# A SwiGLU feed-forward's first product as seven quarter products per block, on x without its norm

## The chip, the core and the metric

The program runs on one core of one Trainium2 chip. The metric is the device time of one execution in microseconds. TensorE does the matmuls into PSUM banks; VectorE (DVE), ScalarE (ACT) and GpSimd (POOL) do everything that is elementwise; the DMAs are issued from SyncE (SP).

## What is computed

Two layers of a decoder trunk on 528 tokens (16 learned ones and 512 of the input) of 1024 channels. Each layer is a feed-forward, a token-mixing part and a second feed-forward, each with an RMS norm before and behind it:

```python
h = h + 0.5 * rms_norm(swiglu(rms_norm(h, g[0]), w_in, w_out), g[1])
...                                   # token mixers: attention, convolution, recurrence, sparse attention
h = h + 0.5 * rms_norm(swiglu(rms_norm(h, g[4]), w_in, w_out), g[5])

def swiglu(x, w_in, w_out):
    gate, up = jnp.split(x @ w_in, 2, axis=-1)
    return (jax.nn.silu(gate) * up) @ w_out
```

`w_in` is 1024 x 5120 and `w_out` 2560 x 1024, all float32. There are four feed-forwards; below they are numbered 1 to 4 in order of time.

## The kernel before

**Numbers.** Activations lie with channels on partitions and tokens in the free dimension: eight tiles of 128 channels, 528 tokens each. A float32 number is used as two float32r parts, hi and lo = value - hi, and a product is hi\*hi + hi\*lo + lo\*hi: three matmuls per 128 channels. The tokens are cut into two halves of 264 columns (256 in feed-forward 4, which drops the learned tokens). So one weight block of 128 output columns costs 8 x 3 = 24 matmuls a half.

**The first product.** The 2560 hidden channels are 20 blocks `j` of 128; a block needs a gate block and an up block of `w_in`. `weight` fetches 1024 columns into a `wraw` buffer (two of them), `wsplit` copies hi on ScalarE (`whi` or `wh`) and subtracts lo on VectorE (`wlo` or `wl`). Three pairs from a pool and three from rings of the mixers (`SPARE`) make six hi/lo pairs that are used in turn. `x` is h times the norm's column of gains; the norm's factor of each token, `R`, is only known later and is multiplied in behind the product. `gated` does that for a half: gate bank times R on VectorE (`ga`), SiLU on ScalarE, up bank times R on VectorE, gate times up on GpSimd, then hi on ScalarE and lo on VectorE into a tile `G`. Blocks 0 to 2 are the lead: they are done at the end of the phase before (`lead`), woven into other work. In feed-forward 4 both halves make one 512-column product in blocks 3 to 19.

**The second product.** The blocks are taken in chunks of 6, 6 and 8 (`CHUNKS`). Behind each chunk its 8 output blocks of 128 channels are made of its `G` tiles and added up in `y`. The last chunk's are the `tail`, woven with the beginning of the next phase; `link` there makes the norm of `y` (`leave`) and the next `x` (`enter`). Feed-forward 4 ends with tokens on partitions instead (`ffn_out_tokens`).

**What sets the order.** Blocks 3 to 19 stand in the program in plain order, and the tile framework's scheduler places each engine's instructions. Tail, mixers and lead are woven by hand: streams are taken by a planner that keeps times per engine (`Weave`), ranks (`RANK`) and a choice of engine per task (`ENG`, `SUMS`); that order is then fixed for TensorE, ScalarE, VectorE and GpSimd. Nearly all instructions carry the line of the recording helper, 252, so the rows are told apart by tile names. Eight PSUM banks stand in three groups: `psu` (2), `psa` (5) and `psn` (1).

Of the kernel before, what the change touches and what calls it, by code (L numbers as in the profile page):

```python
# [9 lines left out]
F32 = mybir.dt.float32  # L10
# [6 lines left out]
P = 128  # L17
# [90 lines left out]
class Weave:  # L108
# [13 lines left out]
    AHEAD = dict(PE=0.0, A=0.19, V=0.0, G=0.3)  # L122
# [255 lines left out]
class Trunk:  # L378
# [6 lines left out]
    LEAD = 3  # L385
    WB = 3
# [6 lines left out]
    ENG = dict(hadd='V', wlead='E', wt='V', wcol='G', wearly='G', wlate='V', wtail='V', wnext='E', gelu='G',  # L393
               geluo='V', gate='G', ct='V', tapsum='E', rfox='E', rconv='V', rlru='E', rdsa='G', lrua='V',
               lrub='E', lruc='V', lrud='V', lrut='G')
    KEPT = ("PE", "A", "V", "G")
    RANK = dict(ev=6.3, late=48.5, weights=10.8, row=100.5, lead=49.3, index=217.3, prep=150.7, scores=13.7,
                dsa=144.3, topk=153.4, fox=42.6, lru=14.4, lrub=59.1, first=81.6, turn0=0, turn1=168.8,
                start0=47.9, start1=229.5, leading=184.0, conv=0, column=99.8, link=0, enter=80.0,
                tail=13.0, small=9.3, next=117.2)  # L400
# [336 lines left out]
    def leave(self, y, acc, c, l, s, factor):  # L737
# [4 lines left out]
        self.norm_rows(acc, R, self.NORMS[0], factor)  # L742
# [30 lines left out]
    def gated(self, G, pg, pu, R, c):  # L773
        nc = self.nc
        w = c.stop - c.start
        tiles = self.tmp(name="ga", many=2)
        t, u = (i[:, :w] for i in tiles)
        nc.vector.tensor_mul(t, pg[:, :w], R[:, c])
        nc.scalar.activation(t, t, AF.Silu)
        nc.vector.tensor_mul(u, pu[:, :w], R[:, c])  # L780
        nc.gpsimd.tensor_mul(u, u, t)
        nc.scalar.activation(G[:, 0, c], u, AF.Copy)
        nc.vector.tensor_sub(G[:, 1, c], u, G[:, 0, c].bitcast(F32))
        self.drop(*tiles)

# [48 lines left out]
    def ffn(self, l, f, w, state, final):  # L834
# [5 lines left out]
        params = self.load_params() if not (l or f) else iter(())  # L840
        for ch, cj in enumerate(CHUNKS):
            base = sum(CHUNKS[:ch])
            Gs = [(self.led[j], 0) for j in range(self.LEAD)] if not ch else []
            for j in range(base + len(Gs), base + cj):
                G = self.at(self.Y[j % 8], [P, 2, T], F32R, name="G")
                ws = [self.weight(wi[:, :, o + j * P : o + (j + 1) * P], KB, P) for o in (0, DFF)]
                next(params, None)
                groups = [[self.half(0, w), self.half(1, w)]] if 2 * w <= 512 else [[self.half(i, w)] for i in range(2)]
                for group in groups:
                    banks = [self.pu(), self.pu()]  # L850
                    for p, hl in zip(banks, ws):
                        self.product(p, hl, KB, x, slice(group[0].start, group[-1].stop))
                    for i, c in enumerate(group):
                        self.gated(G, *(p[:, i * w : (i + 1) * w] for p in banks), R, c)
                Gs.append((G, 0))
            if final:
                self.ffn_out_tokens(l, 5 if f else 1, ch, base, cj, wo, Gs)
# [19 lines left out]
    def tail(self, name, l, f, w, rest, state, pre):  # L877
# [37 lines left out]
        def link(half):  # L915
            wv.wait(f"{name}y{half}")
            c = self.half(half, w)
            update = self.leave(y, sums[half][0], c, l, 5 if f else 1, 0.5)
# [7 lines left out]
    def ffn_out_tokens(self, l, s, ch, base, cj, wo, Gs):  # L926
# [5 lines left out]
        if not ch:  # L932
            self.yt = [self.at(r, [P, D], name="yt") for r in ("fk", "qd", "gl", "cv0")]
            self.grow = self.at("xb", [P, D], name="grow")
            nc.sync.dma_start(self.grow, self.a["norm_g"][l, s].partition_broadcast(P))
        last = ch == len(CHUNKS) - 1
# [1051 lines left out]
```

## Time and profile before

| | us |
|---|---|
| median of 3 runs (2100.37 to 2101.22) | 2100.42 |
| the profiled execution, its own time | 2100.15 |
| its span, first to last instruction | 2098.4 |
| TensorE busy in it | 1989.9 |
| VectorE, ScalarE, GpSimd busy | 1223.5, 900.0, 487.6 |

The span divides into feed-forwards, where TensorE runs without a gap, and the two mixing phases (about 345 to 775 us and 1390 to 1788 us) and one plain link of two feed-forwards (1040 to 1093 us), where all engines share the work. A TensorE instruction's recorded length is longer than its turn, since matmuls follow each other in a pipeline: the turn is a window's length divided by the matmuls in it.

### The profile page before, as it was taken

The numbers are of one execution on the slowest core, as the hardware profiler recorded it, in microseconds if no ns is written. First come the engines' busy times: TensorE is split into PE (matmuls) and PEld (weight loads), VectorE is DVE, ScalarE is ACT, GpSimd is POOL, SyncE is SP. The second block draws the span as 40 slices with busy tenths as digits, with TensorE's granted clock in tenths as the row PEclk, the third lists the DMA queues.
The fourth block names the chain that finished last, engine by engine and source line by source line (L and its number), as shares of the span: only waits on it lengthen the run. The fifth ranks groups of instructions, "written<-read, shape, count | busy, mean of one in ns | idle before, by whom it ended". The sixth has DMA issues, their size and how long they took to land. (4 is left out here: it accounts for less than half of the span.)

```text
span 2098.4 us, 36992 instructions
## 1 busy us (share of the span) xinstructions
PE 1989.9 (95%) x14579; PEld 1880.4 (90%) x14579; DVE 1223.5 (58%) x2831; ACT 900.0 (43%) x1891; POOL 487.6 (23%) x479
## 2 busy tenths in 40 slices
PE   8999999978999999999999999999789898999998
PEld 7999999958878899999989999999678798888886
DVE  4434435899973843444484344458999748434444
ACT  5332223564975533223343322335667655332232
POOL 2101010026764210101121010101376542111121
PEclk9999999969999999999999999999799999999999
DMA  4332323111113233232223323222111132332321
GB/s 138 115 110 71 109 64 94 45 33 51 52 40 115 61 103 108 73 110 71 81 61 114 101 81 102 81 78 51 41 52 36 33 117 61 121 111 90 101 92 50
DMA packets 311078, 168.71 MB, mean 80 GB/s; under 512 B 15968, under 2 KB 302952, under 8 KB 310904
## 3 DMA queue, kind: packets, MB, share of 16 engines
q1 hardware_dynamic: 310616, 165.97, 27.2%
q8 instruction: 114, 1.87, 0.3%
q14 instruction: 60, 0.49, 0.1%
q10 hardware_dynamic: 288, 0.39, 0.1%
HBM read 164.22 MB, written 2.10 MB: 79 GB/s over the span
## 5 line engine op out<-in xcount | busy, mean ns | idle before, releaser
L252 POOL TENSOR_TENSOR ga<-ga 128x264 f32<-128x264 f32 (+1 forms) x160 | 140.3, 878 | 1058.5 <-DVE ga L252 959.2
L252 ACT ACTIVATE whi<-wraw 128x512 fp32r<-128x512 f32 (+4 forms) x258 | 193.0, 761 | 258.2 <-PE psa L252 127.2
L252 ACT ACTIVATE wh<-wraw 128x1024 fp32r<-128x1024 f32 (+3 forms) x190 | 152.5, 813 | 221.7 <-PE psa L252 113.8
L252 PE MATMUL psu<-x,whi 128*128 128x264 f32 (+1 forms) x1108 | 231.3, 302 | 15.8 <-DVE gt L252 10.9
L252 DVE TENSOR_TENSOR wlo<-wraw,whi 128x1024 fp32r<-128x1024 f32 (+3 forms) x166 | 171.3, 1040 | 127.3 <-ACT whi L252 126.5
L252 PE MATMUL psa<-x,whi 128*128 128x264 f32 (+2 forms) x1256 | 239.2, 289 | 2.3 <-DVE ga L252 2.3
L252 DVE TENSOR_TENSOR ga<-psa,R 128x264 f32<-128x264 f32 (+1 forms) x238 | 99.9, 428 | 224.3 <-PE psa L252 218.5
L252 PE MATMUL psa<-x,wh 128*128 128x264 f32 (+2 forms) x1148 | 225.9, 294 | 2.7 <-ACT x L252 2.1
L252 DVE TENSOR_TENSOR wl<-wraw,wh 128x1024 fp32r<-128x1024 f32 (+2 forms) x140 | 153.0, 1098 | 117.4 <-ACT wh L252 116.7
L252 PEld LDWEIGHTS psu<-x,whi 128*128 128x128 f32 x1108 | 184.4, 198 | 20.6 <-DVE gt L252 11.7
L252 PEld LDWEIGHTS psa<-x,whi 128*128 128x128 f32 x1256 | 196.9, 189 | 4.4 <-ACT R L252 2.4
L252 PEld LDWEIGHTS psa<-x,wh 128*128 128x128 f32 x1148 | 182.5, 191 | 6.7 <-ACT x L252 3.0
L252 PE MATMUL psa<-x,wlo 128*128 128x264 f32 (+2 forms) x628 | 181.9, 290 | 0.0
L252 PE MATMUL psu<-x,wlo 128*128 128x264 f32 (+1 forms) x554 | 165.3, 299 | 3.2 <-POOL wlo L252 3.2
L252 PE MATMUL psa<-x,wl 128*128 128x264 f32 (+2 forms) x574 | 167.2, 291 | 0.0
L252 ACT ACTIVATE G<-ga 128x264 fp32r<-128x264 f32 (+1 forms) x160 | 67.5, 422 | 226.8 <-POOL ga L252 225.2
L252 POOL TENSOR_TENSOR wlo<-wraw,whi 128x512 fp32r<-128x512 f32 (+1 forms) x92 | 117.1, 1279 | 115.6 <-ACT whi L252 115.2
L252 PE MATMUL psa<-ycat,wh 128*128 128x264 f32 (+2 forms) x612 | 135.6, 314 | 3.9 <-ACT ycat L252 2.7
L252 POOL TENSOR_TENSOR cv<-cv,cm 128x528 f32<-128x528 f32 x84 | 117.4, 1398 | 55.4 <-ACT cm L252 54.7
L252 DVE TENSOR_TENSOR G<-ga,G 128x264 fp32r<-128x264 f32 (+1 forms) x160 | 78.1, 488 | 86.6 <-ACT G L252 86.2
L252 PE MATMUL psa<-ycat,whi 128*128 128x264 f32 (+2 forms) x552 | 121.6, 314 | 0.0
L252 PEld LDWEIGHTS psa<-x,wlo 128*128 128x128 f32 x628 | 118.7, 189 | 0.9
(306 smaller groups left out, 5129.9 us busy)
## 6 DMA issues: line engine op xcount, KB each, us to landing
wraw<-in_ffn_w_in_dram SPq DMA_DIRECT2D x160, 512.0 KB
wraw<-in_ffn_w_out_dram SPq DMA_DIRECT2D x44, 512.0 KB
wraw<-in_ffn_w_out_dram SPq DMA_DIRECT2D x48, 384.0 KB
wraw<-in_w_in_dram SPq DMA_DIRECT2D x36, 512.0 KB
wraw<-in_w_out_dram SPq DMA_DIRECT2D x180, 64.0 KB
xin<-in_x_dram SPq DMA_DIRECT2D x8, 256.0 KB
wraw<-in_w_out_dram SPq DMA_DIRECT2D x8, 256.0 KB
wraw<-in_w_in_dram SPq DMA_DIRECT2D x4, 256.0 KB
```

The source lines that it names most:

```text
L252: done = call(*args, **kw)
```

## The change

Write one block's first product as a 2 by 2 matrix of token halves a, b and channel halves 1, 2 times a 2 by 2 matrix of weight quarters g1, g2 (gate) and u1, u2 (up), each 512 channels x 128 columns. The old form makes 8 quarter products of 12 matmuls. The new one, for blocks 5 to 19 (`PLAIN` = 5), makes 7: of the quarters themselves and of sums and differences of them, `s1` to `s4`, with `t1` to `t4`, the like of x (`d2`, `d3`, `d4`, and `t1` in place of x's own half b). Blocks 3 and 4 stay plain, now half by half in all four feed-forwards. All of it works on x without `R`; the gate gets `R` before SiLU, the up branch doesn't, so `G` and `y` lack one factor `R` per token, which `link` and `ffn_out_tokens` put into the norm behind. The planner's ranks, engines and the order of the mixers' columns were changed too.

In the diff, `mult` is the 12 matmuls of one quarter product and `keep` a ScalarE copy of a bank. `paired` is an even block, whose four quarters are the halves of two `wraw` buffers, so that two quarters are split by one instruction. `differences` runs once per feed-forward, its lines for k from 0 to 3. `leave` now makes `Rp` as the norm's row times `R` on VectorE, where a ScalarE copy was.

```diff
-    AHEAD = dict(PE=0.0, A=0.19, V=0.0, G=0.3)
+    AHEAD = dict(PE=0.0, A=0.19, V=0.0, G=0.5)
-    ORDER = 'ccvffqgqg'
+    ORDER = 'fccvfqgqg'
-    HOLD = 7
-    SUMS = dict(tail='V', late='V', enter='E')
+    HOLD = 4
+    SUMS = dict(tail='V', late='E', enter='E')
...
@@ gated
-        nc.vector.tensor_mul(u, pu[:, :w], R[:, c])
-        nc.gpsimd.tensor_mul(u, u, t)
+        nc.vector.tensor_mul(u, pu[:, :w], t)
...
@@ ffn
+        state["parts"], state["first"] = self.differences(l, 4 if f else 0, w, state)
...
+            Gs += self.seven(l, f, w, state, wi, range(base + len(Gs), base + cj), params)
@@ quarters
+        if paired:
+            W["g1"], W["g2"] = self.split_pair(raws[0])
+            W["u2"] = self.split_quarter(u2)
+        else:
+            W["g1"] = self.split_quarter(g1)
+            W["g2"] = self.split_quarter(g2)
+            W["u2"] = self.split_quarter(u2)
+        V.tensor_add(u2, u1, u2)
+        V.tensor_sub(u1, g1, u1)
+        V.tensor_sub(g1, u2, g1)
+        V.tensor_sub(g2, g2, g1)
+        if paired:
+            W["s2"], W["s4"] = self.split_pair(raws[0])
+            W["s3"], W["s1"] = self.split_pair(raws[1])
+        else:
...
@@ differences
+            b, d, a, c = scaled(k, 1), scaled(k + 4, 1), scaled(k, 0), scaled(k + 4, 0)
+            V.tensor_sub(a, b, a)
+            V.tensor_sub(b, d, b)
+            V.tensor_sub(d, d, a)
+            V.tensor_sub(c, c, d)
+            put(d, *B["t2"][k])
+            put(b, *B["t3"][k])
+            put(c, *B["t4"][k])
@@ seven
+            mult(g.b[0], g.W["g1"], "a1", True)
+            g.s1 = keep(g.b[0], "s1", "at")
+            mult(g.b[1], g.W["g2"], "a2", True)
+            V.tensor_add(g.s1[:, :w], g.b[1][:, :w], g.s1[:, :w])
+            V.tensor_mul(g.s1[:, :w], g.s1[:, :w], R[:, cs[0]])
+            S.activation(g.s1[:, :w], g.s1[:, :w], AF.Silu)
...
+        def gate(g):
+            mult(g.b[0], g.W["s4"], "b2", False)
+            t = self.tmp(name="ga")
+            V.tensor_mul(t[:, :w], g.b[0][:, :w], R[:, cs[1]])
+            S.activation(t[:, :w], t[:, :w], AF.Silu)
+            G.tensor_mul(g.u4[:, :w], g.u4[:, :w], t[:, :w])
+            self.gate_split(g.G, g.u4, cs[1])
+        def up(g):
+            mult(g.b[2], g.W["u2"], "t4", False)
+            V.tensor_add(g.u2[:, :w], g.b[2][:, :w], g.u2[:, :w])
+            G.tensor_mul(g.u2[:, :w], g.u2[:, :w], g.s1[:, :w])
+            self.gate_split(g.G, g.u2, cs[0])
+        for j in js:
+            g = begin(j)
+            if last:
+                gate(last)
+            mult(g.b[0], g.W["s2"], "t2", False)
+            g.u2 = keep(g.b[0], "u2")
+            if last:
+                up(last)
+            mult(g.b[2], g.W["s3"], "t3", True)
+            mult(g.b[0], g.W["s1"], "t1", False)
+            g.u4 = keep(g.b[0], "u4")
+            V.tensor_add(g.u4[:, :w], g.b[2][:, :w], g.u4[:, :w])
...
@@ link
+            nc.vector.tensor_mul(acc, acc, R[:, c])
+            nc.vector.tensor_mul(acc, acc, R[:, c])
```

How it moves instructions, at three places. VectorE in the third chunk of feed-forward 1 before: one block (two 1024-column `wl`, four products with `R`, two `G`).

```order
L252 TENSOR_TENSOR ga_2932<-psu_2882,R_132 128x264
L252 TENSOR_TENSOR ga_2933<-psu_2883,R_132 128x264
L252 TENSOR_TENSOR G_2869<-ga_2933,G_2869 128x264
L252 TENSOR_TENSOR ga_2990<-psa_2940,R_132 128x264
L252 TENSOR_TENSOR wl_3260<-wraw_3257,wh_3259 128x1024
L252 TENSOR_TENSOR ga_2991<-psa_2941,R_132 128x264
L252 TENSOR_TENSOR wl_3266<-wraw_3263,wh_3265 128x1024
L252 TENSOR_TENSOR G_2869<-ga_2991,G_2869 128x264
```

Now, in the same chunk, 12 rows of about 18 that a block has; `wq` and `wraw` are quarters and their sums, `s1`, `u2`, `u4` the partial gates and ups of blocks 13 to 15.

```order
L254 TENSOR_TENSOR s1_3038<-psa_3023,s1_3038 128x264
L254 TENSOR_TENSOR wlo_3015<-wraw_2996,whi_3014 128x1024
L254 TENSOR_TENSOR s1_3038<-s1_3038,R_132 128x264
L254 TENSOR_TENSOR wl_3157<-wq_3133,wh_3156 128x512
L254 TENSOR_TENSOR u2_2951<-psa_2890,u2_2951 128x264
L254 TENSOR_TENSOR wl_3157<-wq_3131,wh_3156 128x512
L254 TENSOR_TENSOR G_2891<-u4_2993,G_2891 128x264
L254 TENSOR_TENSOR wlo_3019<-wraw_2997,whi_3018 128x1024
L254 TENSOR_TENSOR G_2891<-u2_2951,G_2891 128x264
L254 TENSOR_TENSOR s1_3178<-psa_3163,s1_3178 128x264
L254 TENSOR_TENSOR s1_3178<-s1_3178,R_132 128x264
L254 TENSOR_TENSOR wlo_3277<-wraw_3270,whi_3276 128x1024
```

The splits of later blocks' weights now alternate with additions from PSUM of earlier blocks. TensorE at the same chunk before: the end of a gate product and the start of an up product of one block.

```order
L252 MATMUL psa_2624<-x_139,wh_2614 128x264 x2
L252 MATMUL psa_2624<-x_139,wl_2615 128x264
L252 MATMUL psa_2624<-x_140,wh_2614 128x264 x2
L252 MATMUL psa_2624<-x_140,wl_2615 128x264
L252 MATMUL psu_2625<-x_133,whi_2620 128x264 x2
L252 MATMUL psu_2625<-x_133,wlo_2621 128x264
L252 MATMUL psu_2625<-x_134,whi_2620 128x264 x2
L252 MATMUL psu_2625<-x_134,wlo_2621 128x264
```

Now; `psa_2888` is a bank of block 13, `psa_3022` and `psa_3023` are of block 14, `psa_3163` of block 15, `wh_3002` the new hi of g1 and g2 of block 14.

```order
L254 MATMUL psa_2888<-x_136,wh_2882 128x264 x2
L254 MATMUL psa_2888<-x_136,wl_2883 128x264
L254 MATMUL psa_3022<-x_133,wh_3002 128x264 x2
L254 MATMUL psa_3023<-x_137,wh_3002 128x264 x2
L254 MATMUL psa_3163<-x_137,wh_3140 128x264 x2
L254 MATMUL psa_3163<-x_137,wl_3141 128x264
L254 MATMUL psa_3163<-x_138,wh_3140 128x264 x2
```

Two products of block 14 begin with their hi matmuls and then stand back for a product of block 15. Third, VectorE in the link behind feed-forward 1 before: the last addition to the sum of squares `acc_3653`, and the rows of the norm that are made of it.

```order
L252 TENSOR_TENSOR y_1081<-psu_4312,y_1081 128x264
L252 TENSOR_TENSOR wlo_4300<-wraw_4295,whi_4299 128x344 x2
L252 TENSOR_TENSOR acc_3653<-acc_3653,sq_4369 128x264
L252 SCALAR_TENSOR_TENSOR x_3649<-h_116,gT_112,x_3649 128x264
L252 TENSOR_TENSOR acc_4132<-acc_4132,sq_4398 128x264
L252 TENSOR_TENSOR h_116<-h_116,hn_4199 128x264
L252 TENSOR_SCALAR rows_4406<-psn_4393 88x3
```

Now, from the last addition to `acc_3862` on:

```order
L254 TENSOR_TENSOR acc_3862<-acc_3862,sq_4578 128x264
L254 TENSOR_TENSOR h_116<-h_116,hn_4406 128x264
L254 TENSOR_TENSOR acc_3862<-acc_3862,R_132 128x264
L254 SCALAR_TENSOR_TENSOR x_3858<-h_116,gT_112,x_3858 128x264
L254 TENSOR_TENSOR acc_3862<-acc_3862,R_132 128x264
L254 TENSOR_TENSOR acc_4372<-acc_4372,sq_4612 128x264
L254 SCALAR_TENSOR_TENSOR x_3859<-h_116,gT_112,x_3859 128x264
L254 TENSOR_TENSOR acc_4372<-acc_4372,sq_4628 128x264
L254 TENSOR_SCALAR rows_4633<-psn_4620 88x3
```

Two products of the sum with `R` stand between the last addition and the rows.

## Rows read from the trace of the kernel before

**Rows 1.** The page: engines, then tenths of TensorE in 40 slices.
```profile
PE 1989.9 (95%) x14579; PEld 1880.4 (90%) x14579; DVE 1223.5 (58%) x2831; ACT 900.0 (43%) x1891; POOL 487.6 (23%) x479
...
PE   8999999978999999999999999999789898999998
```

**Rows 2.** Windows by phase: length, busy us (instructions) per engine, clock, DMA.
```profile
core 0: us, PE busy (x) PEld busy (x) DVE busy (x) ACT busy (x) POOL busy (x), PEclk, DMA share, GB/s
0.00:40.00 40.00, 30.38 (x196) 28.97 (x197) 23.14 (x66) 24.18 (x49) 9.40 (x13) 0.92 0.62 180
40.00:345.00 305.00, 305.00 (x2502) 304.81 (x2502) 131.48 (x226) 98.51 (x165) 29.66 (x40) 1.00 0.32 91
345.00:775.00 430.00, 392.14 (x2940) 367.73 (x2939) 328.95 (x915) 247.17 (x586) 169.90 (x155) 0.93 0.22 62
...
1040.00:1093.00 53.00, 47.36 (x358) 45.58 (x357) 46.19 (x123) 25.05 (x60) 11.95 (x10) 0.94 0.21 60
...
1390.00:1788.00 398.00, 351.11 (x2653) 326.34 (x2653) 318.33 (x890) 234.32 (x566) 165.26 (x148) 0.94 0.21 58
```

**Rows 3.** Same view, windows of one matmul width each (256, 264, 512 columns).
```profile
1774.00:1786.00 12.00, 12.00 (x104) 12.00 (x103) 6.61 (x10) 5.17 (x9) 1.47 (x2) 1.00 0.29 82
...
233.50:327.00 93.50, 93.50 (x769) 93.50 (x769) 39.81 (x81) 30.19 (x51) 11.77 (x15) 1.00 0.25 73
1855.00:1915.00 60.00, 60.00 (x261) 48.57 (x260) 28.56 (x42) 20.36 (x33) 12.12 (x10) 1.00 0.34 108
```

**Rows 4.** TensorE groups by shape, whole span: count, busy us, mean recorded ns.
```profile
L252 PE MATMUL psa<-x,whi 128*128 128x264 f32 x1188 | 221.1, 286 | 2.3 <-DVE ga L252 2.3
...
L252 PE MATMUL psu<-ycat,whi 128*128 128x256 f32 x140 | 28.9, 298 | 4.5 <-ACT ycat L252 1.9 <-ACT y L252 1.2 <-DVE y L252 1.2
...
L252 PE MATMUL psa<-x,whi 128*128 128x512 f32 x44 | 13.6, 391 | 0.0
```

**Rows 5.** What TensorE waited for, longest in total first: us, times, longest.
```profile
PE psu L252 <- DVE gt L252: 10.9, 3, 5.8
...
PE psn L252 <- DVE acc L252: 8.8, 4, 3.5
```

**Rows 6.** VectorE groups by shape, 130 to 340 us: busy, mean ns | idle before.
```profile
L252 DVE TENSOR_TENSOR wlo<-wraw,whi 128x1024 fp32r<-128x1024 f32 x13 | 17.3, 1334 | 9.8 <-ACT whi L252 9.8
L252 DVE TENSOR_TENSOR ga<-psa,R 128x264 f32<-128x264 f32 x39 | 16.9, 432 | 41.2 <-PE psa L252 40.6
...
L252 DVE TENSOR_TENSOR G<-ga,G 128x264 fp32r<-128x264 f32 x28 | 12.0, 428 | 22.6 <-ACT G L252 22.6
...
L252 DVE TENSOR_TENSOR wlo<-wraw,whi 128x512 fp32r<-128x512 f32 x8 | 5.4, 689 | 2.4 <-ACT whi L252 2.2
...
L252 DVE TENSOR_TENSOR ls<-ls,ls 128x4 f32<-128x4 f32 x1 | 0.2, 161 | 0.0
```

**Rows 7.** VectorE in order of time: start, length, merged equal instructions.
```profile
33.92 1.29 DVE L252 TENSOR_TENSOR wlo<-wraw,whi 128x512 fp32r<-128x512 f32 x2 [3.79 <-ACT whi L252]
35.13 1.45 DVE L252 TENSOR_TENSOR ga<-psa,R 128x264 f32<-128x264 f32 x4
```

**Rows 8.** GpSimd groups, the same stretch.
```profile
L252 POOL TENSOR_TENSOR ga<-ga 128x264 f32<-128x264 f32 x28 | 21.6, 770 | 207.9 <-DVE ga L252 202.7 <-ACT whi L252 5.1
```

**Rows 9.** ScalarE groups, the same stretch.
```profile
L252 ACT ACTIVATE whi<-wraw 128x1024 fp32r<-128x1024 f32 x12 | 12.7, 1061 | 22.4 <-PE psa L252 14.4 <-PE psu L252 6.4 <-issue 1.6
L252 ACT ACTIVATE G<-ga 128x264 fp32r<-128x264 f32 x28 | 11.9, 425 | 56.2 <-POOL ga L252 56.2
...
L252 ACT ACTIVATE whi<-wraw 128x512 fp32r<-128x512 f32 x8 | 4.7, 624 | 3.7 <-PE psa L252 1.9 <-PE psu L252 1.7 <-DMA wraw<-in_ffn_w_out_dram 0.2
```

**Rows 10.** All engines in order of time, inside one block near 140 us.
```profile
137.87 1.23 DVE L252 TENSOR_TENSOR wl<-wraw,wh 128x1024 fp32r<-128x1024 f32 x1 [0.59 <-ACT wh L252]
...
140.34 0.76 POOL L252 TENSOR_TENSOR ga<-ga 128x264 f32<-128x264 f32 x1 [5.04 <-DVE ga L252]
...
140.76 1.42 DVE L252 TENSOR_TENSOR wl<-wraw,wh 128x1024 fp32r<-128x1024 f32 x1 [0.59 <-ACT wh L252]
```

More of the change, by code (lines that the diff above doesn't have):

```diff
@@ L735, in split, with leave @@
         )
[L737 removed]
+    def leave(self, y, acc, c, l, s, factor, scale=None):
         nc = self.nc
@@ new lines, in seven, with mult, keep, begin @@
+    def seven(self, l, f, w, state, wi, js, params):
+        nc = self.nc
+        V, S, G = nc.vector, nc.scalar, nc.gpsimd
+        self.odd = None
+        B, R = state["parts"], state["R"]
+        cs = [self.half(i, w) for i in range(2)]
+        out = []
+        def mult(bank, quarter, part, start):
+            hi, lo = quarter
+            p = bank[:, :w]
+            for k in range(4):
+                ws = slice(k * P, (k + 1) * P)
+                xh, xl = B[part][k]
+                nc.tensor.matmul(p, hi[:, ws], xh, start=start and k == 0, stop=False, skip_group_check=not start)
+                nc.tensor.matmul(p, hi[:, ws], xl, start=False, stop=False, skip_group_check=not start)
+                nc.tensor.matmul(p, lo[:, ws], xh, start=False, stop=k == 3, skip_group_check=not start)
+        def keep(bank, name, tag="t1"):
+            t = self.tmp(name=name, tag=tag)
+            S.activation(t[:, :w], bank[:, :w], AF.Copy)
+            return t
+        def begin(j):
+            g = SimpleNamespace(W=self.quarters(wi, j), b=[self.pu() for _ in range(3)])
+            next(params, None)
+            if j == self.PLAIN:
+                state["first"]()
+            g.G = self.at(self.Y[j % 8], [P, 2, T], F32R, name="G")
+            mult(g.b[0], g.W["g1"], "a1", True)
[4 more added lines that the diff above has]
+            S.activation(g.s1[:, :w], g.s1[:, :w], AF.Silu)
+            return g
+        def gate(g):
[10 more added lines that the diff above has]
+            self.gate_split(g.G, g.u2, cs[0])
+        last = None
+        for j in js:
[10 more added lines that the diff above has]
+            V.tensor_add(g.u4[:, :w], g.b[2][:, :w], g.u4[:, :w])
+            out.append((g.G, 0))
+            last = g
+        gate(last)
+        up(last)
+        return out
@@ L915, in link @@
         def link(half):
+            c = self.half(half, w)
             wv.wait(f"{name}y{half}")
-            c = self.half(half, w)
-            update = self.leave(y, sums[half][0], c, l, 5 if f else 1, 0.5)
+            acc = sums[half][0]
+            nc.vector.tensor_mul(acc, acc, R[:, c])
+            nc.vector.tensor_mul(acc, acc, R[:, c])
+            update = self.leave(y, acc, c, l, 5 if f else 1, 0.5, R[:, c])
             self.enter(name, half, c, state["x"], state["R"], *pre, update)
@@ L935, in ffn_out_tokens @@
             nc.sync.dma_start(self.grow, self.a["norm_g"][l, s].partition_broadcast(P))
+            p = self.ps()
+            self.Rt = [self.tiny([P, 4], f"Rt{i}") for i in range(2)]
+            for b in blocks:
+                nc.tensor.matmul(p[:, b : b + 1], R[0:1, NM + b * P : NM + (b + 1) * P], self.ones[0:1, 0:1],
+                                 start=True, stop=True)
+            V.tensor_copy(self.Rt[0], p[:, :4])
+            V.tensor_mul(self.Rt[1], self.Rt[0], self.Rt[0])
         last = ch == len(CHUNKS) - 1
```

150 lines of the change are left out of this document (122 added, 28 removed).

## The prediction

> **What bounds the kernel now.** I read the page first: TensorE is busy 95% of the span, VectorE 58%, and TensorE's tenths are 9 in nearly every slice [rows 1]. Then the windows by phase [rows 2]. From 40 to 345 us TensorE is busy all 305.00 us at granted clock 1.00, VectorE 131.48; in the mixing phases TensorE still does 392.14 of 430 and 351.11 of 398 us. What it waits for adds up to little: the longest entry is 10.9 us [rows 5]. So in the feed-forwards every matmul that goes saves its turn, until another engine needs as long as TensorE for a block. The step that needs care is therefore the second one: VectorE's time for a block.
>
> The turn is (window + one recorded length) / matmuls in it, since the count takes in those that reach over the edges. For 264 columns (93.5 + 0.29) / 769 = 0.122 us, for 256 columns (12 + 0.30) / 104 = 0.118, for 512 columns (60 + 0.39) / 261 = 0.231 [rows 3, 4].
>
> **TensorE: what goes.** Feed-forwards 1 to 3 have 15 blocks each that drop from 96 to 84 matmuls: 45 x 12 x 0.122 = 65.9 us. In feed-forward 4, 17 blocks of 48 matmuls of 512 columns took 816 x 0.231 = 188.5 us; now 2 x 96 + 15 x 84 = 1452 matmuls of 256 columns take 1452 x 0.118 = 171.3 us, 17.2 less. Sum 83.1 us. The profiled execution took 2100.15 us (the median of the runs is 0.27 above), so 2017 us if nothing else ends later.
>
> **VectorE: does it keep up?** A block of the new form takes TensorE 84 x 0.122 = 10.25 us. VectorE's recorded lengths are 1.23 us for 1024 columns undisturbed [rows 10], 0.69 for 512 and 0.43 for 264 [rows 6], but instructions in a row overlap: two of 512 columns take 1.29 us together, four of 264 take 1.45 [rows 7], so a step is 0.60 and 0.34, some 0.09 under the recorded length, and I take 1.14 for 1024. An even block has three splits of 1024 columns, one of 512, four sums of 512 and seven instructions of 264 (s1 twice, u4, u2, the gate, two G): 3 x 1.14 + 5 x 0.60 + 7 x 0.34 = 8.8 us; an odd one 11 x 0.60 + 7 x 0.34 = 9.0. That is 87% of TensorE's 10.25; before, VectorE was busy 39.81 us of the 93.5 us of eight blocks, 43% [rows 3]. By full recorded lengths it is 10.2 and 10.6 us. ScalarE's share is smaller: 3 x 1.06 + 0.62 or 7 x 0.62 us of hi copies, and seven instructions of 264 columns at 0.42 [rows 9], some 7 us.
>
> GpSimd does two products a block, 0.77 us each [rows 8], now among far more VectorE work. What they do to each other one place shows: a split of 1024 columns that began 0.42 us after a GpSimd product took 1.42 us, not 1.23 [rows 10], 0.19 more. Twice 0.19 makes 9.3 us a block, still hidden. If all of GpSimd's 1.54 us were added it would be 10.4, or 0.2 over TensorE. The Trainium skill (SBUF — State Buffer, "Who interferes with whom") says that a VectorE instruction with two SBUF inputs and a GpSimd one that reads SBUF exclude each other, the second fully blocked until the first is done; by that the whole 1.54 us counts, while the one place above shows only a part of it.
>
> I take 0.2 us a block exposed, 60 x 0.2 = 12 us, since the order leaves VectorE little freedom: its splits for a later block stand between additions that wait for TensorE. What softens it: six hi/lo pairs hold 1.7 blocks of 3.5 pairs, which VectorE fills ahead during the second products, and those need it far less.
>
> **The smaller parts.**
> - At the end of each run of new blocks (12 of them) the last G comes after an addition, a GpSimd product, a hi copy and a lo: 0.43 + 0.77 + 0.42 + 0.43 = 2.05 us [rows 6, 8, 9], and TensorE has 15 or 21 matmuls that don't need it, 1.8 or 2.6 us. With handoffs I take 0.4 us each, 5 us.
> - The differences: 28 instructions each on VectorE (9.6 us) and ScalarE, once per feed-forward, beside 23.4 us of plain blocks 3 and 4. There VectorE also has their splits (4.6), their gates (12 x 0.34 = 4.1) and block 5's quarters (6.6): 24.9 in all, covered by the lead's second half and the 48 matmuls of block 5 that come before `t1`; TensorE also has second products to fill with, and the order has put some there. `t1` itself must wait for block 4. 0 to 2 us, taken as 0.5, four times: 2 us.
> - The links: two products with R ahead of the norm's rows, 2 x 0.43 us, and Rp by VectorE for a copy. TensorE waited for `acc` 8.8 us in 4 times [rows 5], so half of these show; three links at 1 us: 3 us.
> - The end: two tiny VectorE instructions at 0.16 us [rows 6] on the last block of tokens and four tiny matmuls earlier: 0.5 us.
> - Fetches: a block's 1 MB comes in four pieces for two. In the first 40 us the queue moved 180 GB/s [rows 2], 5.8 us a block, and a fetch may start one block ahead: nothing. If the buffers came free late it would show as the third rival.
> - `gated` now multiplies the up bank by the gate on VectorE and needs no GpSimd product: one handoff fewer ahead of G in the lead and blocks 3 and 4. TensorE runs without gaps there [rows 2], so nothing is gained.
> - The mixing phases. Their columns, ranks and engines are reordered, and 57 weight splits leave GpSimd, mostly for VectorE (57 x 0.60 = 34 us over both phases, where VectorE is idle 101 and 80 us [rows 2]). No row of before can show that order. Bounds from the nearest rows: TensorE is idle 38 and 47 us there and 6 in the plain link [rows 2]; a tenth either way is 9 us. I take 0.
>
> Sum: 2017 + 12 + 5 + 2 + 3 + 0.5 = 2039.5; I say 2040 us.
>
> **The rivals.**
> *VectorE sets the pace (slower).* If the overlap of 0.09 is lost in waiting for handoffs and GpSimd's products count in full, a block costs 10.4 + 1.54 = 11.9 us on VectorE. Then each of 60 blocks loses 1.7 us: 2017 + 102 + 10 = 2129 us. It decides from 10.25 + 83 / 60 = 11.6 us a block on. For it: the count of instructions, and splits that stand behind additions. Against: the weights made ahead, and second products between the runs in which VectorE catches up (in chunks of 6 and 8 blocks it starts 1.7 blocks, some 11 us of splits, ahead). By the skill's rule of exclusion alone, with overlap kept, the loss is the 12 us that I have.
> *The pairs recycle too late (faster, half of it lost).* A block's last quarter, u2, is read only in the next block's products; its pair can then be refilled, by a copy and a split of 1.06 + 1.23 us for 1024 columns [rows 9, 10]. The order shows TensorE starting hi matmuls of a block and standing back for another's, so new weights are just in time there. If 1 us of the 2.3 shows once a block: 2017 + 60 + 10 = 2087 us.
> *All of it, and a little from the mixers (faster still).* Nothing exposed and a tenth of the 91 us of idle TensorE gained: 2017 + 5 - 9 = 2013 us.
> That the change wouldn't save the matmuls is no case: the order of after holds 12 matmuls a quarter product and seven of them.
>
> **How the numbers follow.** The forecast (2025 to 2060) 0.58; all of it (2005 to 2025) 0.18; late pairs (2060 to 2096) 0.14; within 0.2%, which is about what a measurement of this kernel can tell from no change, 0.03, where the losses happen to be the 83 us; VectorE's pace 0.07. Faster 0.58 + 0.18 + 0.14 = 0.90. The range 2010 to 2080 holds the forecast, most of the second case and about half of the third; it leaves out some 0.19.
>
> **What would show it.** Right: between 130 and 345 us TensorE again busy nearly throughout, matmuls of 264 columns at 0.122 us a turn, the eight-block run of a feed-forward some 82 us for 93.5, VectorE above eight tenths in it; feed-forward 4 shorter by 15 us or so. Wrong: TensorE's waits led by `wl`, `wlo` or `s1` of VectorE with tens of us; VectorE's splits of 512 columns well over 0.69 us; a lower granted clock in the feed-forwards; or a mixing phase longer than 430 or 398 us by more than 10.

## The result: slower by one per cent

The changed kernel takes 2121.51 us (median of 4 runs, 2118.78 to 2123.78) where the kernel before took 2100.39 in the same session: ratio 1.0099, 95% interval 1.0082 to 1.0117. The forecast was 2040 and faster. The profiled execution took 2118.78 us, its span 2117.0.

The page of the changed kernel, the lines that answer to [rows 1]:

```profile
PE 1957.4 (92%) x14683; PEld 1852.8 (88%) x14683; DVE 1553.2 (73%) x3556; ACT 1095.2 (52%) x2397; POOL 442.2 (21%) x390
...
PE   8999989978989899998999999899789898999998
```

TensorE is busy 32.5 us less than before, but the span is 18.6 us longer. The tenths that were all 9 in the feed-forwards now have 8s.

Where it went, I read by windows that begin and end with a matmul that every version has. A *feed-forward stretch* runs from the last matmul of the first chunk's second product to the last one of the tail; a *mixer stretch* from there over the mixing phase to the next feed-forward's first second product. The four feed-forward stretches of the kernel before, their sum (length, then busy time per engine):

```profile
sum 990.20, PE 985.35 PEld 939.80 DVE 461.17 ACT 306.65 POOL 117.06; mean PE 246.34 PEld 234.95 DVE 115.29 ACT 76.66 POOL 29.26
```

The same four of the changed kernel (columns as in [rows 2]):

```profile
124.40:375.20 250.80, 236.24 (x1886) 231.82 (x1885) 183.07 (x348) 117.17 (x231) 33.39 (x30) 0.99 0.31 88
812.10:1068.30 256.20, 236.94 (x1863) 231.26 (x1862) 178.25 (x319) 112.23 (x224) 35.83 (x31) 0.99 0.30 87
1184.40:1436.70 252.30, 237.01 (x1884) 231.70 (x1883) 178.48 (x328) 113.97 (x228) 31.42 (x29) 0.99 0.31 88
1867.40:2106.80 239.40, 226.81 (x1545) 208.37 (x1544) 166.03 (x302) 106.94 (x219) 43.01 (x39) 0.99 0.28 86
sum 998.70, PE 937.00 PEld 903.15 DVE 705.83 ACT 450.32 POOL 143.65; mean PE 234.25 PEld 225.79 DVE 176.46 ACT 112.58 POOL 35.91
```

Before, TensorE was idle 990.20 - 985.35 = 4.9 us in them, now 61.7. The matmuls did go: the first stretch has 1886 for 2055, 14 blocks x 12. By the prediction's turns these 14 blocks save 3 x 14 x 12 x 0.122 = 61.5 us in feed-forwards 1 to 3 and 14 x (48 x 0.231 - 84 x 0.118) = 16.5 in the fourth, 78 us, so the stretches should take 912; they take 998.7. Of the 86 us that are lost, 57 are added idle time. The rest stands inside "busy", which fell by 48 us only: after a gap the first matmul is recorded with 0.4 us where its turn is 0.12, and the granted clock is 0.99 where it was mostly 1.00. The trace's clock records have 17.1 us at 0.5 in these stretches, for 3.4 before; half of the difference is 6.8 us; 77 gaps at some 0.27 us are another 21, an estimate from the two lengths.

The two mixer stretches take 436.9 + 430.7 = 867.6 us for 854.1, another 13.5. The plain link (117.4, now 116.1 us), the start (127.8, now 124.4) and the end (8.9, now 10.2) make up the rest of the 18.6.

So there are two questions: who keeps TensorE waiting in the feed-forwards, and why phases that the change hardly touches got longer. This table has every run that is told of below; the stretches come from its one profiled execution. The kernel before took 2100.4 to 2101.6 us in the sessions, and each ratio is to its own session.

| kernel | median us | ratio to before, interval | four feed-forward stretches | two mixer stretches |
|---|---|---|---|---|
| before | 2100.4 | | 990.2 | 854.1 |
| after | 2121.5 | 1.0099 [1.0082, 1.0117] | 998.7 | 867.6 |
| no_seven | 2116.6 | 1.0072 [1.0057, 1.0087] | 987.8 | 870.5 |
| no_sums | 2062.5 | 0.9814 [0.9800, 0.9829] | 941.4 | 868.3 |
| no_gpsimd_product | 2091.1 | 0.9943 [0.9922, 0.9964] | 972.9 | 866.3 |
| five_pairs | 2089.7 | 0.9944 [0.9929, 0.9959] | 971.4 | 864.7 |
| five_other_pair | 2084.7 | 0.9925 [0.9911, 0.9940] | 959.8 | 867.9 |
| five_pairs_new_tables_vector_product | 2081.2 | 0.9906 [0.9888, 0.9923] | 965.0 | 863.4 |
| other_five_vector_product | 2081.6 | 0.9908 [0.9893, 0.9922] | 960.5 | 865.9 |
| old_tables | 2131.8 | 1.0144 [1.0123, 1.0165] | 1011.1 | 874.7 |
| five_pairs_old_tables | 2095.3 | 0.9968 [0.9955, 0.9982] | 974.8 | 871.8 |
| five_pairs_vector_product | 2090.0 | 0.9943 [0.9922, 0.9964] | 973.5 | 864.1 |
| before_new_tables | 2096.9 | 0.9986 [0.9976, 0.9997] | 990.4 | 854.0 |
| factor_in_gate_only | 2117.1 | 1.0078 [1.0063, 1.0093] | 989.0 | 877.3 |
| factor_in_link_only | 2119.2 | 1.0088 [1.0073, 1.0103] | 989.3 | 869.3 |
| plan_bias | 2111.4 | 1.0050 [1.0034, 1.0066] | 988.5 | 870.9 |
| plan_gpsimd_ahead | 2101.8 | 0.9999 [0.9990, 1.0009] | 988.2 | 857.0 |
| plan_scalar_ahead | 2109.5 | 1.0044 [1.0029, 1.0059] | 988.8 | 865.9 |

### The profile page after: what moved, and what is told of

The parts are those of the page before. It is cut to its first block, busy times and chain, and to the rows that moved or that the text cites. A ratio compares the mean times of both kernels' runs of the same rounds, so it can differ in the third digit from the quotient of the medians.

```text
span 2117.0 us, 38278 instructions
## 1 busy us (share of the span) xinstructions
PE 1957.4 (92%) x14683; PEld 1852.8 (88%) x14683; DVE 1553.2 (73%) x3556; ACT 1095.2 (52%) x2397; POOL 442.2 (21%) x390
## 4 chain that ended last, share of the span: by engine, by line
PE 62%; DVE 22%; ACT 6%; POOL 3%; issue 3%; DMA 3%; SPq 1%; DVEq 0%; ACTq 0%; POOLq 0%
PE psa L254 40%; PE psu L254 21%; DVE wlo L254 2%; DVE wl L254 2%; DVE msel L254 2%; DVE wraw L254 2%; PE psn L254 2%; ACT whi L254 1%; POOL u L254 1%; DMA wraw<-in_ffn_w_out_dram 1%; DVE wq L254 1%; POOL cv L254 1%; DVE lra L254 1%; DVE acc L254 1%; DVE cv L254 1%
## 5 line engine op out<-in xcount | busy, mean ns | idle before, releaser
L254 DVE TENSOR_TENSOR wlo<-wraw,whi 128x512 fp32r<-128x512 f32 (+4 forms) x181 | 158.6, 885 | 97.2 <-ACT whi L254 90.7
L254 DVE TENSOR_TENSOR wl<-wraw,wh 128x1024 fp32r<-128x1024 f32 (+3 forms) x162 | 158.3, 985 | 75.0 <-ACT wh L254 73.8
L254 ACT ACTIVATE wh<-wraw 128x512 fp32r<-128x512 f32 (+3 forms) x180 | 140.9, 796 | 138.1 <-PE psa L254 49.4
L254 PE MATMUL psa<-x,wh 128*128 128x264 f32 (+1 forms) x776 | 157.0, 295 | 11.9 <-DVE h L254 3.9
L254 PE MATMUL psa<-x,whi 128*128 128x264 f32 (+1 forms) x836 | 165.8, 293 | 1.1 <-ACT u L254 1.1
L254 POOL TENSOR_TENSOR cv<-cv,cm 128x528 f32<-128x528 f32 x84 | 119.5, 1423 | 60.0 <-ACT cm L254 58.8
L254 PE MATMUL psa<-x,wlo 128*128 128x264 f32 (+1 forms) x418 | 120.7, 291 | 0.0
L254 PE MATMUL psa<-x,wl 128*128 128x264 f32 (+1 forms) x388 | 112.7, 292 | 0.0
L254 PE MATMUL psa<-d,whi 128*128 128x264 f32 (+1 forms) x536 | 101.7, 285 | 3.9 <-ACT wh L254 2.0
L254 PE MATMUL psa<-G,wh 128*128 128x264 f32 x524 | 99.4, 285 | 0.1
L254 PEld LDWEIGHTS psu<-x,wlo 128*128 128x128 f32 x506 | 97.7, 194 | 0.8 <-issue 0.6
```

The lines of the kernel that those rows point to most:

```text
L254: done = call(*args, **kw)
```

## What the trace of after shows in one block

What TensorE waited for over the whole span of after, to be held against [rows 5]:

```profile
PE psa L254 <- ACT wh L254: 21.8, 15, 3.4
PE psn L254 <- DVE lra L254: 17.4, 3, 8.3
PE psa L254 <- ACT u L254: 8.3, 13, 1.8
PE psu L254 <- DVE gt L254: 7.7, 3, 6.2
PE psu L254 <- ACT G L254: 6.9, 3, 3.2
```

The new leader is `wh`, a weight's hi copy on ScalarE. But the name of the releaser isn't yet the cause, as one place shows. VectorE of after in order of time (start, length), in feed-forward 2:

```profile
834.05 0.68 DVE L254 TENSOR_TENSOR wq<-wq 128x512 f32<-128x512 f32 x1
834.66 0.42 DVE L254 TENSOR_TENSOR s<-psu,s 128x264 f32<-128x264 f32 x1
835.00 0.67 DVE L254 TENSOR_TENSOR wlo<-wq,whi 128x512 fp32r<-128x512 f32 x1
835.60 0.68 DVE L254 TENSOR_TENSOR wraw<-wraw 128x512 f32<-128x512 f32 x1
836.20 0.42 DVE L254 TENSOR_TENSOR ga<-psa,R 128x264 f32<-128x264 f32 x1
836.54 0.68 DVE L254 TENSOR_TENSOR wq<-wq 128x512 f32<-128x512 f32 x1
837.14 0.42 DVE L254 TENSOR_TENSOR s<-s,R 128x264 f32<-128x264 f32 x1
837.49 0.68 DVE L254 TENSOR_TENSOR wlo<-wq,whi 128x512 fp32r<-128x512 f32 x1
838.09 0.42 DVE L254 TENSOR_TENSOR u<-psa,u 128x264 f32<-128x264 f32 x1
838.43 0.91 DVE L254 TENSOR_TENSOR wlo<-wq,whi 128x512 fp32r<-128x512 f32 x1
839.26 1.24 DVE L254 TENSOR_TENSOR wraw<-wraw 128x512 f32<-128x512 f32 x1
```

ScalarE and TensorE there (the same view, each its own row):

```profile
836.36 1.06 ACT L254 ACTIVATE wh<-wraw 128x1024 fp32r<-128x1024 f32 x1 [0.44 <-issue]
```

```profile
837.47 0.51 PE L254 MATMUL psa<-d,wh 128*128 128x264 f32 x2 [1.69 <-ACT wh L254]
```

VectorE has no gap at all. At 835.60 it makes the sum whose hi copy follows on ScalarE at 836.36, and TensorE, idle since 835.78, begins with that copy at 837.47. But ahead of that sum, at 835.00, VectorE did a split of the *next* block's weights, one half of `wlo_10210` by the program's order, and of that TensorE has no use before 841.00. The `wq` sum at 834.05 is the next block's as well. Without these two, 0.60 us each by [rows 7], VectorE would have come to the sum 1.2 us sooner. So the engine that is late here is VectorE, the name in the wait is ScalarE's, and the reason is as much VectorE's fixed order as its load.

Three of the 15 waits of that row are of this kind (5.3 us of the 21.8). In six others the copy stood, in ScalarE's own fixed order, behind an instruction that had waited for VectorE (5.8 us), in four behind one that had waited for a GpSimd product (8.7), and in two it waited for TensorE (2.0). One of the four, where the sum had been ready for 0.96 us (the second row is the copy):

```profile
865.90 0.42 ACT L254 ACTIVATE G<-u 128x264 fp32r<-128x264 f32 x1 [1.51 <-POOL u L254]
866.23 1.04 ACT L254 ACTIVATE wh<-wraw 128x1024 fp32r<-128x1024 f32 x1
```

So ScalarE's order hands on what VectorE and GpSimd are late with.

GpSimd's products of this place show the second thing:

```profile
837.87 0.91 POOL L254 TENSOR_TENSOR u<-u,ga 128x264 f32<-128x264 f32 x1 [6.52 <-ACT ga L254]
838.75 1.20 POOL L254 TENSOR_TENSOR u<-u,s 128x264 f32<-128x264 f32 x1
```

Over the whole span, the page's group (busy, mean ns):

```profile
L254 POOL TENSOR_TENSOR u<-u,ga 128x264 f32<-128x264 f32 (+1 forms) x60 | 67.5, 1125 | 976.6 <-ACT ga L254 976.6
```

Beside them the VectorE instructions of 512 columns at 838.43 and 839.26 take 0.91 and 1.24 us, for 0.68 in the rows above. At other places of after the same is seen: 1.25 us for 0.68, 0.98 for 0.42. The lengths are those of two engines that take turns. The split at 838.43 begins when 0.35 us of the first product are left, the second product (838.75) when 0.59 of that split are left, the sum (839.26) when 0.69 of that product are left; each is longer by this rest less some 0.13 us. The addition at 838.09 lies inside the first product as well and takes its usual 0.42; it reads one of its inputs from PSUM.

It is so in the whole trace of after. Inside 107 of the 120 products begins a VectorE instruction that reads two tiles in SBUF; 97 times it is longer by what is left of the product, less 0.10 to 0.16 us, and the other ten, not longer at all, went ahead of a product that still had 1.3 us or more to go, more than its own 0.77. Of the VectorE instructions that read PSUM, 42 overlap a product, and none is longer by more than 0.014 us. One product so costs VectorE up to 0.57 us, and takes itself 1.1 us in the mean, not the 0.77 of [rows 8]. The 0.19 us of [rows 10] was no smaller price: that split began with 0.34 us of the product left.

The Trainium skill (SBUF — State Buffer, "Who interferes with whom") has the second of two such instructions fully blocked until the first is done. The trace agrees, in both directions: beside the 97 VectorE instructions above, 85 of the 94 products that began inside one of VectorE's are longer by the rest of it, less 0.12 to 0.17 us, and the other nine by more.

## Experiments on the feed-forwards

The theory after this reading: VectorE's work, what GpSimd does to it, and the order in which it is fixed keep TensorE waiting. The rivals: the planner's new tables, or the norm's factor behind.

**Without the seven products.** The diff of the change kept, but blocks 5 to 19 as before: 8 quarter products, 512 columns in feed-forward 4.

```diff
...
-            Gs += self.seven(l, f, w, state, wi, range(base + len(Gs), base + cj), params)
...
+                    for p, hl in zip(banks, ws):
+                        self.product(p, hl, KB, x, slice(group[0].start, group[-1].stop))
...
```

> Blocks 3 to 19 as before (gate and up in 8 quarter products, 512 columns in feed-forward 4), with the norm's factor still put behind and with the changed ranks and engines. If all of the missing gain lies in the blocks of seven, this takes 2100 us, within 4. If the reordered mixers and the links cost what the two traces differ by outside the blocks (12 us of TensorE time lost in the mixing phases, some in the tails), 2108 to 2115 us. A theory that the new ranks help the mixers has it under 2095 us.

Measured 2116.6 us, just above the second theory's range. Its feed-forward stretches are those of before, 987.8 us with 3.6 idle, while its mixer stretches take 870.5, as long as after's 867.6 or longer. So the longer mixers don't come from the seven products, and the seven products by themselves, 2116.6 to 2121.5, lost 5 us where they were to gain 78 in the stretches.

**Without the sums of weights.** Four VectorE instructions of 512 columns per block are left out, so the quarters themselves are used in place of sums and differences.

```diff
-        V.tensor_add(u2, u1, u2)
-        V.tensor_sub(u1, g1, u1)
-        V.tensor_sub(g1, u2, g1)
-        V.tensor_sub(g2, g2, g1)
```

> The changed kernel without the four sums and differences of weight quarters (the products go on with the quarters themselves, so the output is not the reference's): four VectorE instructions of 512 columns less in each of 60 blocks, 2.4 us a block, TensorE's work the same. Theory A (VectorE's own work is late with the weights): TensorE's loss in the blocks, 1.2 us each, goes mostly away, 2060 to 2080 us. Theory B (the hi/lo pairs come free too late): pairs are freed as before, so under 12 us is gained, 2108 to 2120 us.

**Without GpSimd's products.** The two lines `G.tensor_mul` of `gate` and `up` are left out, so `G` lacks one factor.

> The changed kernel without the two GpSimd products of gate and up in each of 60 blocks (the output is not the reference's). Theory A with exclusion (a GpSimd product adds half of its length or more to the VectorE instruction beside it, 1.1 us a block): 2075 to 2100 us. If the two do not disturb each other, only the ends of the runs are shorter: 2112 to 2120 us.

Measured 2062.5 and 2091.1 us. The sums over the four feed-forward stretches of no_sums, then of no_gpsimd_product:

```profile
sum 941.40, PE 918.55 PEld 897.29 DVE 580.62 ACT 452.21 POOL 120.44; mean PE 229.64 PEld 224.32 DVE 145.15 ACT 113.05 POOL 30.11
```

```profile
sum 972.90, PE 931.00 PEld 902.54 DVE 666.54 ACT 451.23 POOL 12.25; mean PE 232.75 PEld 225.63 DVE 166.64 ACT 112.81 POOL 3.06
```

57 us come back when VectorE has 125 us less to do there, and 26 when GpSimd is silent. (Without the sums the hi copies also wait for nothing that VectorE makes; the run doesn't separate that from the work.) ScalarE's work is the same in both, and the mixer stretches stay where they were. In the first run of no_sums TensorE doesn't wait at all, and its turn is 55.20 / 452 = 0.122 us, the prediction's:

```profile
124.80:180.00 55.20, 55.20 (x452) 54.89 (x452) 34.92 (x66) 33.31 (x65) 7.72 (x9) 1.00 0.32 91
```

VectorE is busy 63% there. The same run in after has it at 46.28 of 57.20, 81%:

```profile
124.40:181.60 57.20, 54.68 (x437) 53.30 (x436) 46.28 (x83) 30.98 (x62) 9.32 (x9) 1.00 0.31 87
```

437 matmuls are 5.2 blocks, which would be 8.9 us of VectorE a block. But VectorE had made weights of these blocks before the window began. Matched row by row with the program, the rows of all 60 blocks occupy VectorE for 9.96 us a block (a row counts to its end, or to the start of the next one if that comes first), and for 9.32 in no_gpsimd_product: GpSimd's products add 0.6. The prediction had 8.9 and, for GpSimd, 0.38. TensorE takes 10.25 us, and in the window above VectorE is idle for 10.9 us while TensorE waits. So VectorE is not the bound by its load alone.

**Five weight pairs for six.** If the order matters, working less far ahead should help: with one pair fewer, the splits of a later block can't stand so far ahead, since their buffer isn't free.

```diff
 def quarter
-            self.wturn = (self.wturn + 1) % (self.WB + len(SPARE))
+            self.wturn = (self.wturn + 1) % (self.WB + len(SPARE) - 1)
```

> The blocks of seven use five of the six hi/lo pairs, all else the same. Theory B (pairs are what is scarce): a pair less is felt at once, 2150 us or more. Theory A (VectorE is late, pairs wait for it rather): under 15 us slower, 2120 to 2135 us.

Measured 2089.7 us: 32 us faster than after, with the same work. Neither theory had a gain. The feed-forward stretches, summed:

```profile
sum 971.40, PE 934.01 PEld 906.40 DVE 712.96 ACT 455.12 POOL 139.59; mean PE 233.50 PEld 226.60 DVE 178.24 ACT 113.78 POOL 34.90
```

VectorE does 713 us of work where it did 706, and TensorE is idle 37.4 us where it was 61.7. What TensorE waited for in the first run of feed-forward 2, after (812.1 to 877.6 us) and then five_pairs (807.5 to 861.7 us):

```profile
PE psa L254 <- ACT wh L254: 4.8, 3, 2.1
PE psa L254 <- ACT u L254: 1.1, 2, 0.5
PE psu L254 <- DVE wl L254: 0.3, 1, 0.3
```

```profile
PE psa L254 <- ACT whi L254: 0.4, 1, 0.4
```

Fewer buffers, the same work, less waiting: that speaks for the order and against the load alone. It could still be that one pair, which lies in the mixers' ring `wide`. So the next run keeps that one and leaves out another (beside the line above):

```diff
-                          for i, r in enumerate(SPARE[self.wturn - self.WB]))
-            self.split_last[self.wturn] = lo
+                          for i, r in enumerate(SPARE[self.wturn - self.WB + 1]))
+            self.split_last[self.wturn + (self.wturn >= self.WB)] = lo
```

> The changed kernel with five hi/lo pairs for the quarters, like five_pairs (2089.7 us), but the ring pair that is left out is the first of the mixers' three, not the last. If fewer pairs are what helps, since VectorE's fixed order then can't run ahead to a later block: 2085 to 2097 us. If it is that one buffer (its ring, or what else waits for it) that cost the 32 us: about the changed kernel's 2121 us.

Measured 2084.7 us, so it is the number of pairs and not the buffer. VectorE indeed works less far ahead: matched with the program, VectorE's 420 splits of quarters end in the median 9.5 us before their first matmul in after and 5.1 in both of these kernels, while the rows of a block occupy VectorE as long (9.96 and 9.90 us). That this helps by way of the order is argued; no run changed VectorE's order with six pairs, and none had four.

**GpSimd's products on VectorE.** In five_pairs, `G.tensor_mul` in `gate` and `up` becomes `V.tensor_mul`; then the same on the other five pairs.

> Five pairs, the changed kernel's own tables, and the two products of each block that GpSimd did now on VectorE. If exclusion between the two engines costs VectorE more than the 2 x 0.43 us that it takes over: 2080 to 2087 us, the 5 us of five_pairs_vector_product over five_pairs_old_tables taken off five_pairs. If the pairs alone were the trouble, no change from 2090 us. If VectorE is still the bound after the pairs are fewer: slower, 2090 + 60 x 0.4 = some 2110 us.

> The changed kernel with five pairs as in five_other_pair (2084.7 us) and the blocks' two GpSimd products on VectorE. If the two measures add: 2075 to 2082 us. If it is GpSimd's exclusion alone that was left, the same as five_pairs_new_tables_vector_product, 2081 us; if the order of the mixers decides, 2070 to 2095.

Measured 2081.2 and 2081.6 us. Taking over 0.86 us of work a block cost VectorE nothing in sum, since it waits for no product any more; its busy time in the stretches, 711.17 us, is that of five_pairs:

```profile
sum 965.00, PE 928.89 PEld 902.54 DVE 711.17 ACT 451.77 POOL 12.43; mean PE 232.22 PEld 225.63 DVE 177.79 ACT 112.94 POOL 3.11
```

Its instructions have their undisturbed lengths again, in the first run (mean ns behind the comma) after has

```profile
L254 DVE TENSOR_TENSOR wl<-wq,wh 128x512 fp32r<-128x512 f32 x10 | 7.7, 800 | 2.3 <-ACT wh L254 2.2
```

and this kernel

```profile
L254 DVE TENSOR_TENSOR wl<-wq,wh 128x512 fp32r<-128x512 f32 x7 | 4.7, 686 | 0.0
```

On the pairs of five_pairs this gained 8.6 us; on the other five 3.1, where the runs of the two kernels overlap (2082.1 to 2087.6 and 2078.7 to 2083.2), so what it is worth there is open. Both kernels beat the one before by 0.9%, 19 and 20 us, and are the fastest of those that leave nothing out.

## Experiments on the tables and the mixers

**The tables.** `AHEAD`, `ORDER`, `HOLD`, `SUMS`, `ENG` and `RANK` of before in the changed kernel (old_tables), and those of after in the kernel before (before_new_tables):

```diff
-    ORDER = 'fccvfqgqg'
-    HOLD = 4
+    ORDER = 'ccvffqgqg'
+    HOLD = 7
...
```

> The changed kernel with the ranks, engines, column order, HOLD, SUMS and AHEAD of the kernel before. If those tables cost what no_seven lost against the kernel before (16 us, all of it in the mixing phases and the plain link), this takes 2105 us, within 5. If the norm's factor behind costs it, it stays at 2118 to 2123 us.

> The kernel before with the changed ranks, engines and column order alone. Tables at fault: 2112 to 2118 us. Norm's factor behind at fault: 2098 to 2103 us.

Measured 2131.8 and 2096.9 us: the new tables are better in both kernels, by 10 and 4 us; for old_tables neither theory had that. They are not what made the change slow. Two more kernels had old tables and five pairs, the second with the products on VectorE:

> Both: five of six pairs in the blocks of seven, and the old tables. If the two causes are separate the gains add: 2121 - 32 - 16 = 2073 us. If five pairs was a chance of one order, which another order undoes, 2095 us or more.

> As five_pairs_old_tables, and the two GpSimd products of a block are done by VectorE, 0.34 us each by its step. Exclusion costs VectorE about 0.5 us a product in the trace (1.25 us for 0.68), so 0.3 us a block is gained and the chain to the last G is shorter: 15 to 30 us less than five_pairs_old_tables. If exclusion cost nothing, VectorE would have 0.7 us more a block: 10 to 40 us more.

Measured 2095.3 and 2090.0 us. The first is where the expectation put a chance of one order, but it counted on old tables that gain 16 us, and they cost 10: against old_tables, five pairs gain 37 us here too. The products on VectorE gain 5 more, where 15 to 30 were expected and the runs overlap (2089.3 to 2102.7 and 2084.3 to 2093.3).

**The factor behind, in two halves.** From before_new_tables (2096.9) to no_seven (2116.6) only the norm's factor moved behind, and that cost 20 us, 16.5 of it in the mixer stretches. One half of it alone, `gated`:

```diff
-        nc.vector.tensor_mul(u, pu[:, :w], R[:, c])
-        nc.gpsimd.tensor_mul(u, u, t)
+        nc.vector.tensor_mul(u, pu[:, :w], t)
```

> The kernel before with the new tables (2096.9 us), and of the norm's factor behind only the gate's part: the up bank is multiplied by the gate on VectorE, with no factor and no GpSimd product; the links don't put the factor back, so that part of the computation is left out. If the 20 us that no_seven lost against those tables come from the mixers' planned order, which changes with the gate's stream: 2110 to 2117 us. If they come from the links' products: 2095 us.

And the other half alone, `link` and `leave` as in the change with before's `gated`:

> The same kernel with only the other part: the links and the last norm multiply by the factor, the gate keeps its product with the factor and GpSimd's product (so the factor is counted twice). If the links' two products and the norm's row on VectorE cost the 20 us: 2110 to 2117 us. If the gate's stream does: 2097 to 2101 us, the 3 us that the prediction gave the links.

Measured 2117.1 and 2119.2 us. Each half alone costs as much as both together. Prices of work don't behave like that, and what the halves have in common is that the planner places the mixers anew.

**The order alone.** Three kernels with exactly the instructions of before_new_tables and one planner constant moved a little, such as

```diff
-    BIAS = 0.46
+    BIAS = 0.47
```

> The kernel before with the new tables (2096.9 us) and the planner's constant BIAS at 0.47 for 0.46: the same instructions, another order in the mixing phases. If the 20 us of the factor behind are that two edits made the planner place the mixers anew, three such kernels spread from 2097 to 2117 us, with at least one over 2105. If each edit has its own price, all three stay within 2092 to 2102 us.

> The same with the planner's AHEAD for GpSimd at 0.48 for 0.5. Luck of the order: anywhere from 2097 to 2117 us; an own price of the edits: 2092 to 2102 us.

> The same with the planner's AHEAD for ScalarE at 0.20 for 0.19. Luck of the order: anywhere from 2097 to 2117 us; an own price of the edits: 2092 to 2102 us.

Measured 2111.4, 2101.8 and 2109.5 us, 14.5, 4.9 and 12.6 over before_new_tables, with no edit of the work at all. Where it lies, two kernels show in the mixer stretches without the second product at their end. before_new_tables, then plan_bias:

```profile
379.90:773.60 393.70, 362.06 (x2671) 334.84 (x2670) 309.32 (x876) 230.69 (x549) 144.27 (x132) 0.93 0.21 57
1425.00:1817.40 392.40, 353.79 (x2510) 319.74 (x2509) 312.53 (x874) 231.20 (x548) 148.32 (x128) 0.94 0.21 61
```

```profile
378.40:778.00 399.60, 369.71 (x2671) 339.37 (x2670) 308.18 (x877) 231.82 (x549) 144.81 (x131) 0.92 0.20 56
1432.30:1835.60 403.30, 361.71 (x2510) 326.37 (x2509) 313.08 (x873) 230.39 (x548) 144.54 (x129) 0.92 0.21 60
```

16.8 us more, and TensorE's busy time grew by 15.6 of them, with the same matmuls: it ran longer at the lower clock. Summed from the trace's clock records, it was granted 0.5 for 95.6 us of these windows in before_new_tables, 126.3 in plan_bias; half of the difference is 15.4 us. In factor_in_gate_only it was 136.5 us, and half of that difference, 20.5, stands beside 23.1 us of length. One of the stretches in plan_bias, with what was ahead of it (TensorE's busy time first, granted clock third from the right):

```profile
537.00:541.00 4.00, 4.00 (x34) 3.98 (x33) 2.78 (x6) 1.90 (x4) 3.15 (x3) 1.00 0.25 72
541.00:544.40 3.40, 2.51 (x27) 2.31 (x25) 3.40 (x11) 0.73 (x2) 1.59 (x1) 1.00 0.13 37
544.40:561.50 17.10, 17.10 (x64) 12.19 (x64) 11.02 (x38) 7.90 (x22) 5.52 (x4) 0.50 0.00 0
561.50:570.00 8.50, 8.50 (x72) 7.31 (x70) 7.57 (x26) 7.83 (x21) 5.50 (x5) 1.00 0.01 2
```

TensorE is without a gap up to 541, then idle for 0.89 us before 543.32, and from 544.4 on it is granted half the clock, 1.2 GHz, for 17 us in which it is busy throughout. before_new_tables has no such stretch between 500 and 590 us. If the gap is what brought the clock down, 0.89 us of waiting cost 8.5 more. That isn't shown: most matmuls around it are small ones (106 x 64), and no run separates the two.

The order moves such places, but it doesn't settle the clock. Ten executions of plan_bias, all of one order, took 2103.9 us (mean granted clock 0.974) to 2117.9 (0.965); the traced one took 2116.2. before_new_tables has 2094.0 (0.975) to 2102.6 (0.971), traced 2098.2. So the two traces are further apart than the medians, and it is the medians that price an order.

Not all of it is so explained. factor_in_link_only was at the low clock 13.6 us longer than before_new_tables, worth 6.8 of the 15.1 us that these windows got longer, and plan_scalar_ahead the same 13.6, for 11.7. And the three edits cost 20 to 22 us where moving a constant cost 5 to 14.5. By the medians, up to 14.5 of the 20 us need no edit of the work; whether the remaining 5 are the edits' own or more of the same, these runs don't tell.

## Why the prediction was wrong, by its steps

- **TensorE's saving** was right: the matmuls went, 0.122 us a turn held where nobody else was late (no_sums). Of the 83 us, 78 belong to the four feed-forward stretches.
- **VectorE's load**, 8.8 to 9.0 us a block and 9.3 with GpSimd's share, was low: 9.32 with GpSimd silent and 9.96 with its products. The steps of 0.60 and 0.34 us are right where VectorE has no gap (834 to 838 us above); a row before a gap counts some 0.09 more, and GpSimd's share is 0.6 for 0.38. By the prediction's own rule, which counts only what goes over 10.25 us, this loses nothing.
- **"0.2 us a block exposed" is the step that failed.** The prediction allowed 11 us for 56 blocks and 3 for the ends of eight runs in the stretches, so they should have become 64 us shorter; they became 8.5 longer. The loss is 86 us, 1.5 a block, ends of runs and tails included. The words behind the figure, that the order leaves VectorE little freedom since splits for a later block stand between additions, named the mechanism; the working then took only the excess of load over TensorE's 10.25 us, as if an engine below 100% could always do first what is needed first. Waiting for an engine that takes its work in a fixed order was priced as if it only began at 100%.
- **What softens it** was wrong in sign. Six pairs, 1.7 blocks ahead, were to help; the sixth pair cost 32 to 37 us. It lets the fixed order put a later block's splits ahead of what TensorE needs next, as at 835 us; that this is how it costs them is argued, not shown.
- **GpSimd against VectorE**: the one place was read as a part of the exclusion. It was the whole of it, for a split that began when the product was half over; in after what is left of a product is longer in the mean (0.55 us where a VectorE instruction waited). Taking GpSimd out was worth 26 us in the stretches of after; ScalarE had waited for its products as well.
- **The ends of runs**: 12 x 0.4 us. TensorE waited for `G` only at the third runs' ends of feed-forwards 1 to 3, in all 9.4 us for ScalarE's hi half and 1.2 for VectorE's lo; at the other ends the trace has no such wait. About twice the 5 us in sum, and not the main loss.
- **The mixers, 0 with bounds of 9 us**: 13.5. The bound was a tenth of TensorE's idle time; but it isn't the idle time that changed most, it is how long TensorE ran at the lower clock: 119.5 us of after's mixer stretches, for 99.0 before, worth 10 of the 13.5. With the work unchanged the stretches ranged from 854 to 871 us in single executions.
- **The links** at 1 us each: the plain link's stretch got 1.3 us shorter, and 1.5 of block 5's saving lies in it, so 0.2 is left for its link. The other two lie in the mixer stretches and can't be told apart there.
- **The rivals.** The time is next to that of "VectorE sets the pace", 2129, but not for its reason: that asked for 11.6 us of VectorE work a block, and there are 9.96. It is nearer to the mechanism of "late pairs", weights just in time; there one pair more would have helped, and it did harm. What the prediction said would show it wrong did show: waits led by a weight, 512-column splits at 800 ns in the mean for 690.

## What to carry to other kernels

An engine that takes its work in a fixed order isn't hidden because it has less to do than the busiest one: ask for every piece what stands ahead of it, and whether that is needed sooner. More buffers of lookahead can make it worse; one pair fewer was worth 32 to 37 us here and two products a block taken from GpSimd up to 9 more. And where a planner places the work, an edit can move phases that it doesn't touch: before a few per mille are put down to an edit, the same work should be run in two or three other orders, which here gave 2097 to 2111 us.

## What was not expected of the hardware

VectorE and GpSimd took exact turns: a VectorE instruction with both inputs in SBUF was longer by the rest of the GpSimd product beside it (97 of 107 in after, up to 0.57 us), a product by the rest of VectorE's instruction, and VectorE instructions that read PSUM weren't touched (42, at most 0.014 us). After an idle time of 0.89 us, TensorE was granted 0.5 of its clock for 17 us, though it was busy throughout these. The same matmuls were granted the low clock for 96 us of the two mixing phases in one traced execution and for 126 in another order's, and one order's executions were up to 14 us apart.
